# An fp32 hybrid-attention layer on one core: the first rows read in another order, two squares on VectorE, the second mean's chain given out sooner, and twelve weights kept as halves

## The chip, the cores and the metric

The kernel runs on one core of one Trainium2 chip. The metric is the device time of one execution in microseconds. Five engines work side by side, each on its own in-order queue: TensorE (PE, with PEld for its weight loads), VectorE (DVE), ScalarE (ACT), GpSimd (POOL) and SyncE (SP), which here only issues DMAs; GpSimd issues DMAs as well.

## The reference

One layer for 2048 prompt tokens and 32 sample tokens of width 1024 (2080 columns), all in float32:

```python
h = rmsnorm(x, ln_g)                                   # needs the mean of x*x of each token
q, k, v, gate_a, b_gate, c_gate, u_in, gate_c, merge_a, merge_c = split(h @ w_in)
attn, new_k, new_v = attend(rope(rmsnorm(q)), rope(rmsnorm(k)), v, sink)   # windows of 3 chunks of 64
y_a = (attn * silu(gate_a)) @ w_attn_out               # W_A
y_c = (b_gate * conv3(c_gate * u_in) * silu(gate_c)) @ w_conv_out          # W_B
r = x + (sigmoid(merge_a) * y_a + sigmoid(merge_c) * y_c) @ w_o            # O
out = r + sigmoid(r @ w_ple_gate) * (p @ w_ple_proj)   # PG and pp
```

It returns out, the rolled key and value rows, and the last two rows of the convolution's input.

## The kernel before, in words

**Arithmetic.** A float32 product is made of three fast products: each operand is split into a high half (a cast, on ScalarE) and a low half (the operand minus its high half, on VectorE), and TensorE adds high by high, high by low and low by high. The big products go over 2 by 2 blocks with 7 products instead of 8 (Strassen's scheme); for that, sums of four blocks of a weight are made on VectorE and kept in DRAM (`ws`, `qs`), and sums of blocks of the tokens are made the same way (`s`, `T`, `X`).

**Stages.** Times are those of the profiled execution.

- 0 to about 85 us, the start. The rows of p, four pieces of W_pp (`wpp_piece`, L931: raw tile `wppr`, halves `wpp_h` and `wpp_l`), the constants and x (`x_row`, L943) are loaded by SyncE. TensorE makes pp = p @ W_pp for blocks 0 and 1 while the mean of the first 512 tokens is worked out, then the first products of W_in. `x_row(j, k)` loads rows k of part j, squares them on ScalarE (`sq`) and adds the squares on VectorE into `sq_0`. When eight are added, `stats(j)` (L962) goes: eight one-column matmuls `pr` on TensorE, `rs` on VectorE, the power -1/2 on GpSimd, the diagonal `dg` on VectorE, four transposes `rps` on TensorE, a copy `rb` on ScalarE, and then the norms `b<-b,cst,rb`, x's halves and, for the second part (j = 1), the block sums (`combos` L1017, `make0` L1028). `sums0` (L1043) makes the weight sums of the first group and stores four of them.
- To about 440 us, the products of W_in in the first half of the tokens. They follow a list of steps, each of a dozen 128x512 matmuls (L1255 on). Beside them run extra pieces of work tied to the numbers of steps: sums of quads of W_o and W_pg (`quad_sums`, L375, at the steps of `sums_at`).
- About 440 to 860 us, the second half's products. Rows of x come back from DRAM (`refill`, L603; `refill_set`, L629: `xr`), weights come as `wr`. In this stage `half_steps` (L389) loads weights of W_A and the four sums of each O column one at a time, splits them (cast on ScalarE, subtraction on VectorE) and stores both halves in DRAM; `stored(key)` (L410) tells later stages that such a weight is loaded as halves and needs no split.
- 861 us to the end, attention (`attention`, L1399), yB, yA, the rest of pp, and the products O and PG (`big_x` L1705, `run_big` L1863; their sums are the tile `b`).

**What sets the order.** In the start and the last stage a planner runs while the program is written out. It has a clock of its own (`now`), a price for each instruction (`cost`, L104), and a queue of pieces of work with a due time and a rank. `go(g, us, need, rank)` (L184) gives out a generator; whenever TensorE's written work has moved on, `due` (L197) issues those that are due and whose buffers are free, by rank. An Engine object records every call, so all the planner's instructions have the line L160. Loads of the start come from a list, `todo_loads` (L1086), one after the other as SyncE's queue is free. In the last stage `next_loads` (L1994) orders weight loads and splits ahead of the product that runs; a weight is split once its load has landed by the planner's clock and ScalarE is not booked beyond a limit (L2044). Pieces of attention are begun `PRE` = 8 us ahead of their place (L2107). In between (85 to 860 us) the order is that of the list of steps.

Each engine runs what it got in that order, so a piece that waits holds what is behind it on its own engine.

Lines that the steps below touch (numbers of the profile):

```python
112            if key == "G":
113                return 2.03 if kw.get("op") == ALU.pow else 0.35 + 0.0021 * n
946        yield {"k": 1, "@": "S"}
948        eS.activation(out=sq, in_=v[:, :q0], func=AF.Square, scale=1.0 / 32.0)
953            yield {"@": "V"}
954            eV.tensor_tensor(out=acc0[j], in0=acc0[j], in1=sq, op=add)
958        if ready[j] == 8:
959            go(stats(j), now[0] + 1.8, None, j * 2 - 3)
1055        for p, i in WS.items():
1056            eG.dma_start(out=wsum[0][:, i], in_=sums[0][p])
```

## Time and profile before

| | us |
|---|---|
| three runs | 1509.11, 1510.27, 1509.16 |
| median | 1509.16 |
| the profiled execution | 1508.07 |
| its span, first to last instruction | 1506.0 |
| TensorE busy in it | 1489.3, 9553 matmuls |
| VectorE, ScalarE, GpSimd busy | 1210.7, 803.7, 399.0 |
| mean granted clock of TensorE | 0.998 |

How to read the rows quoted below. A row of the timeline is: start, length, engine, line, operation, output <- inputs (tile names without their numbers), shape, and how many such instructions follow each other; in brackets the idle time ahead of it and what ended that. The length of a group of several is from the first's start to the last's end. A matmul's length includes its way through the array, so the pace is read from start to start. A row of the waits is: who waited, for what, total, times, the longest. "SPq" is SyncE's queue: the issue of a DMA, not its transfer.

### The profile page before, as it was taken

The page shows a single profiled execution, that of the slowest core. Times are in us where ns is not written, and L with a number is a line of the kernel's source. Part 1 is how long each engine was busy: PE and PEld are TensorE (multiplying, and loading weights), DVE is VectorE, ACT ScalarE, POOL GpSimd, SP SyncE. Part 2 cuts the span into 40 slices and gives each one's busy share as a digit, 9 for nine tenths or more (in the row PEclk, how much of TensorE's full clock was granted, in tenths as well). Part 3 has the DMA queues.
Part 4 walks back from the last instruction along what each step waited for, and adds up shares of the span by engine and source line. Part 5 has one row for each costly group of instructions (what it writes and reads, how often), then busy time and mean ns, then how long its engine had stood idle before and what let it go on. Part 6 is the DMA issues. An engine that isn't in the chain of part 4 may idle for free.

```text
span 1506.0 us, 28005 instructions
## 1 busy us (share of the span) xinstructions
PE 1489.3 (99%) x9553; PEld 1348.6 (90%) x9553; DVE 1210.7 (80%) x2308; ACT 803.7 (53%) x1910; POOL 399.0 (26%) x582
## 2 busy tenths in 40 slices
PE   9999999999999999999999999999999999999998
PEld 7878888888889999999999989998888788999998
DVE  7897887885579788799976878778899999676777
ACT  8453244344457655434455646687765686342453
POOL 2133332332211443433323311113232202211201
PEclk9999999999999999999999999999999999999999
DMA  9469886898777987533578885687988959989959
GB/s 353 154 246 348 314 291 221 276 347 271 253 274 256 340 292 262 186 127 122 153 243 312 288 270 181 210 253 218 302 207 272 240 157 258 312 247 283 256 168 286
DMA packets 206670, 378.34 MB, mean 251 GB/s; under 512 B 24896, under 2 KB 58496, under 8 KB 206528
## 3 DMA queue, kind: packets, MB, share of 16 engines
q1 hardware_dynamic: 160608, 258.30, 52.6%
q0 software_dynamic: 36272, 100.44, 22.2%
q10 hardware_dynamic: 9648, 17.83, 3.2%
q8 instruction: 75, 1.23, 0.3%
q14 instruction: 67, 0.55, 0.1%
HBM read 246.53 MB, written 130.04 MB: 250 GB/s over the span
## 4 chain that ended last, share of the span: by engine, by line
PE 91%; DMA 4%; DVE 2%; ACT 1%; issue 1%; POOL 0%; SPq 0%; DVEq 0%; ACTq 0%; POOLq 0%
PE b L160 21%; PE a L654 8%; PE a L651 7%; PE a L649 7%; PE yB L160 6%; PE yA L160 5%; PE la L787 5%; PE c L651 4%; PE c L649 4%; PE c L654 4%; PE lc L787 2%; PE pp L160 2%; PE O L160 2%; PE S L160 2%; PE PT L160 1%; PE lb L787 1%
## 5 line engine op out<-in xcount | busy, mean ns | idle before, releaser
L160 PE MATMUL b<-xb_h,w 128*128 128x264 f32 (+1 forms) x1344 | 310.7, 322 | 1.4 <-DVE at L160 1.4
L160 PEld LDWEIGHTS b<-xb_h,w 128*128 128x128 f32 x1344 | 222.7, 188 | 19.5 <-DVE at L160 1.9
L651 PE MATMUL a<-x_l,w 128*128 128x264 f32 (+1 forms) x744 | 228.2, 320 | 0.0
L649 PE MATMUL a<-x_h,w 128*128 128x264 f32 (+1 forms) x744 | 227.4, 320 | 0.2 <-ACT w L231 0.2
L160 PE MATMUL b<-xb_l,w 128*128 128x264 f32 (+1 forms) x672 | 216.6, 322 | 0.0
L654 PE MATMUL a<-x_h,w 128*128 128x264 f32 (+1 forms) x744 | 199.7, 321 | 0.9 <-DVE w L232 0.9
L231 ACT CAST w<-wr 128x512 fp32r<-128x512 f32 (+1 forms) x180 | 110.5, 619 | 96.2 <-PE c L654 34.9
L232 DVE TENSOR_TENSOR w<-wr,w 128x512 fp32r<-128x512 f32 (+1 forms) x180 | 133.2, 748 | 29.6 <-ACT w L231 28.0
L649 PEld LDWEIGHTS a<-x_h,w 128*128 128x128 f32 x744 | 139.9, 188 | 11.3 <-ACT w L231 0.4
L651 PEld LDWEIGHTS a<-x_l,w 128*128 128x128 f32 x744 | 140.0, 188 | 10.9
L654 PEld LDWEIGHTS a<-x_h,w 128*128 128x128 f32 x744 | 124.0, 188 | 11.9 <-DVE w L232 1.2
L160 PEld LDWEIGHTS b<-xb_l,w 128*128 128x128 f32 x672 | 126.4, 188 | 8.5
L160 ACT CAST w<-wr 128x512 fp32r<-128x512 f32 x120 | 73.6, 622 | 98.4 <-PE b L160 51.5
L787 PE MATMUL la<-x_h,w 128*128 128x264 f32 x516 | 111.3, 285 | 1.6 <-ACT w L231 1.6
L651 PE MATMUL c<-x_l,w 128*128 128x512 f32 (+1 forms) x336 | 110.9, 340 | 0.0
L649 PE MATMUL c<-x_h,w 128*128 128x512 f32 (+1 forms) x336 | 110.5, 339 | 0.0
L231 ACT CAST w<-a 128x512 fp32r<-128x512 f32 x82 | 49.8, 620 | 98.6 <-DVE a L364 33.2
L654 PE MATMUL c<-x_h,w 128*128 128x512 f32 (+1 forms) x336 | 100.1, 339 | 0.0
L160 DVE TENSOR_TENSOR w<-wr,w 128x512 fp32r<-128x512 f32 x120 | 83.6, 705 | 18.0 <-ACT w L160 17.7
L848 DVE SCALAR_TENSOR_TENSOR u<-u,c 128x264 f32<-128x264 f32 (+1 forms) x125 | 59.5, 507 | 42.8 <-ACT u L843 26.1
L160 PE MATMUL yB<-ycs_h,w 128*128 128x264 f32 (+1 forms) x384 | 91.0, 325 | 0.0
L160 PE MATMUL yA<-ac_h,w 128*128 128x264 f32 (+1 forms) x384 | 90.5, 323 | 0.0
(443 smaller groups left out, 3889.7 us busy)
## 6 DMA issues: line engine op xcount, KB each, us to landing
wr<-in_wu SPq DMA_DIRECT2D x161, 256.0 KB, 4.8
a<-in_wu SPq DMA_DIRECT2D x116, 256.0 KB, 5.3
wr<-ws SPq DMA_DIRECT2D x74, 256.0 KB, 4.0
w<-o SPq DMA_DIRECT2D x32, 512.0 KB, 4.7
ws<-a POOLq DMA_DIRECT2D x63, 256.0 KB, 4.3
w<-wa SPq DMA_DIRECT2D x16, 512.0 KB, 5.3
wr<-qs SPq DMA_DIRECT2D x32, 256.0 KB, 4.0
qs<-a POOLq DMA_DIRECT2D x24, 256.0 KB, 5.8
```

Source lines behind the costliest of these rows:

```text
L160: return f(**kw)
L231: nc.scalar.copy(out=hi, in_=src)
L232: nc.vector.tensor_tensor(out=lo, in0=src, in1=hi.bitcast(F32), op=sub)
L649: nc.tensor.matmul(out=ps[:, :cn], lhsT=w[:, 0, k], rhs=x[0][:, c0:c0 + cn], start=first and k == 0, stop=False, skip_group_check=True)
L651: nc.tensor.matmul(out=ps[:, :cn], lhsT=w[:, 0, k], rhs=x[1][:, c0:c0 + cn], start=False, stop=False, skip_group_check=True)
L654: nc.tensor.matmul(out=ps[:, :cn], lhsT=w[:, 1, k], rhs=x[0][:, c0:c0 + cn], start=False, stop=k == 3, skip_group_check=True)
L787: nc.tensor.matmul(out=ps[:, :m], lhsT=w[:, a, k], rhs=r[:, cols], start=q in "ABG" and j == 0 and e == 0, stop=j == 1 and e == 2, skip_gr ...
L848: nc.vector.scalar_tensor_tensor(out=t[:, c0:c0 + cn], in0=t[:, c0:c0 + cn], scalar=-1.0, in1=ps[:, :cn], op0=mul, op1=sub)
```

## The change

Six edits:

- **The start's loads.** The fourth W_pp piece goes ahead of x rows 6 and 7 instead of behind them, the two rows of p's second block ahead of the first two weights, and all W_pp pieces get rank -3. The squares of x rows 2 and 5 of the first part are made on VectorE (x / 1024 times x) instead of ScalarE.
- **The second mean.** `stats(j)` is given out 0.3 us instead of 1.8 us after the last sum; this holds for both means. The planner's price for the power on GpSimd falls from 2.03 to 1.1.
- **The stores of the weight sums** go out one at a time, each when GpSimd is free and with rank 2, instead of four in a row.
- **Twelve weights as halves.** The weights (O, 1), (O, 4) and (PG, 1) of each of four columns n are loaded, split and stored as halves beside the steps of the first half, from the products of group 14 to the last group; in the last stage each of them is loaded as halves, 512 KB, with no split. A piece's four parts come 4 steps and 1 step ahead of its place, at it, and 0.4 steps behind.
- **The split condition.** A weight that is needed next may be split though ScalarE is booked up to 5.0 us ahead (before 1.5).
- **Attention** begins its first three pieces 11 us ahead instead of 8.

```diff
+H0 = 14
@@ cost
-            return 2.03 if kw.get("op") == ALU.pow else 0.35 + 0.0021 * n
+            return 1.1 if kw.get("op") == ALU.pow else 0.35 + 0.0021 * n
@@
+    RAW = {1: 0, 4: 1}
+    halves0 = {(x, n, p): dram.tile([P, 2, 4 * P], F32, tag=f"r{x}{n}_{p}", name=f"r{x}{n}_{p}")
+               for x, p in ((UO, 1), (UO, 4), (UPG, 1)) for n in range(4)}
@@ half_steps
+            elif key in halves0:
+                u, e = key[0] + key[1] + 4 * (key[2] == 4), RAW[key[2]]
+                nc.sync.dma_start(out=t.rearrange("p (a b) -> p a b", a=4), in_=wu[u, :, 4 * e:4 * e + 4, :])
@@ stored
+        if key[0] == "B" and key[1] == 0:
+            return halves0.get(key[2:])
@@ wpp_piece
-        go(hilo0(...), None, None, -3 if h < 2 else -1)
+        go(hilo0(...), None, None, -3)
@@ x_row
-        yield {"k": 1, "@": "S"}
+        vector = j == 0 and k in (2, 5)
+        yield {"k": 1, "@": "V" if vector else "S"}
         sq = row(f"sq{j}_{k}")[:, :q0]
-        eS.activation(out=sq, in_=v[:, :q0], func=AF.Square, scale=1.0 / 32.0)
+        if vector:
+            eV.scalar_tensor_tensor(out=sq, in0=v[:, :q0], scalar=1.0 / 1024.0, in1=v[:, :q0], op0=mul, op1=mul)
+        else:
+            eS.activation(out=sq, in_=v[:, :q0], func=AF.Square, scale=1.0 / 32.0)
...
-            go(stats(j), now[0] + 1.8, None, j * 2 - 3)
+            go(stats(j), now[0] + 0.3, None, j * 2 - 3)
@@ sums0
-        for p, i in WS.items():
-            eG.dma_start(out=wsum[0][:, i], in_=sums[0][p])
+        kept = dict(sums[0])
+
+        def keep():
+            for p, i in WS.items():
+                eG.dma_start(out=wsum[0][:, i], in_=kept[p])
+                yield {"@": "G"}
+        go(keep(), None, None, 2)
@@ todo_loads
-    todo_loads += [({}, (-2, x_row(0, k))) for k in range(3, 8)] + [({"wf": 1}, (-1, wpp_piece(3)))]
-    todo_loads += [({"wf": 1}, (0, raw0(i))) for i in range(2)] + [({"tmp": 1}, (0, p_row(1, k))) for k in range(2)]
+    todo_loads += [({}, (-2, x_row(0, k))) for k in range(3, 6)] + [({"wf": 1}, (-2, wpp_piece(3)))]
+    todo_loads += [({}, (-2, x_row(0, k))) for k in (6, 7)] + [({"tmp": 1}, (-1, p_row(1, k))) for k in range(2)]
+    todo_loads += [({"wf": 1}, (0, raw0(i))) for i in range(2)]
@@ the list of steps
+    gen0 = [half_steps(*x) for x in halves0.items()]
+    first0, last0 = at_step[0, H0, 7], at_step[0, G - 1, 5]
+    pitch0 = (last0 - first0) / (len(gen0) - 1)
+    at0 = sorted((first0 + pitch0 * j + lag, j) for j in range(len(gen0)) for lag in (-4, -1, 0, 0.4))
...
+        while at0 and at0[0][0] <= i:
+            next(gen0[at0.pop(0)[1]])
@@ next_loads
-                if landed.get(i, 1e9) > now[0] or busy["S"] >= now[0] + (0.3 if i > used[0] + 2 else 1.5):
+                if landed.get(i, 1e9) > now[0] or busy["S"] >= now[0] + (0.3 if i > used[0] + 2 else 1.5 if i > used[0] + 1 else 5.0):
@@ attention's begin
-        begin.append((max(0.0, t - PRE), lambda e=e, t=t: go(attention(e, t), None, {"z": 1, "tmp": 2})))
+        begin.append((max(0.0, t - (PRE if e > 2 else 11.0)), lambda e=e, t=t: go(attention(e, t), None, {"z": 1, "tmp": 2})))
```

What this does to the written order is shown at three places. (The changed file's lines stand one to thirteen further down: L161 is L160, L618 is L609, L353 is L352, L455 is L446.)

VectorE in the first 17 us, before. `wpp_l` is the low half of a W_pp piece (`wppr_260` the third, `wppr_272` the fourth), `sq_0` the sum of squares:

```order
L160 TENSOR_TENSOR sq_0_302<-sq_0_302,sq_1_307 128x512
L160 TENSOR_TENSOR sq_0_302<-sq_0_302,sq_2_311 128x512
L160 TENSOR_TENSOR wpp_l<-wppr_260,wpp_h 128x512
L160 TENSOR_TENSOR sq_0_302<-sq_0_302,sq_3_325 128x512
L160 TENSOR_TENSOR sq_0_302<-sq_0_302,sq_4_356 128x512
L160 TENSOR_TENSOR sq_0_302<-sq_0_302,sq_5_363 128x512
L160 TENSOR_TENSOR sq_0_302<-sq_0_302,sq_6_368 128x512
L160 TENSOR_SCALAR cst<-cst 128x64
L160 TENSOR_TENSOR sq_0_302<-sq_0_302,sq_7_374 128x512
L160 TENSOR_TENSOR wpp_l<-wppr_272,wpp_h 128x512
```

The same place after (`wppr_272` is now the third piece, `wppr_280` the fourth; `b_2` and `b_5` are x rows):

```order
L161 SCALAR_TENSOR_TENSOR sq_2_323<-b_2_270 128x512
L161 TENSOR_TENSOR sq_0_314<-sq_0_314,sq_1_319 128x512
L161 TENSOR_TENSOR sq_0_314<-sq_0_314,sq_2_323 128x512
L161 TENSOR_TENSOR wpp_l<-wppr_272,wpp_h 128x512
L161 TENSOR_TENSOR sq_0_314<-sq_0_314,sq_3_337 128x512
L161 SCALAR_TENSOR_TENSOR sq_5_375<-b_5_278 128x512
L161 TENSOR_TENSOR sq_0_314<-sq_0_314,sq_4_368 128x512
L161 TENSOR_TENSOR sq_0_314<-sq_0_314,sq_5_375 128x512
L161 TENSOR_TENSOR wpp_l<-wppr_280,wpp_h 128x512
L161 TENSOR_TENSOR sq_0_314<-sq_0_314,sq_6_389 128x512
L161 TENSOR_SCALAR cst<-cst 128x64
L161 TENSOR_TENSOR sq_0_314<-sq_0_314,sq_7_397 128x512
```

Two squares are new in this queue, and the fourth piece's low half stands two sums further up. On TensorE the eight matmuls `pr` move one place down, behind the fourth of the fourth piece's matmuls instead of the third.

VectorE at the second mean, 47 to 57 us, before. `rs`, `dg` are the mean's chain, `s` sums of products, `w` low halves of weights, `b` the norm of x rows:

```order
L160 TENSOR_SCALAR rs_1_720<-pr_1_721 128x4
L523 MEMSET rs_0_2062 128x5
L160 TENSOR_TENSOR s_0_642<-2_0_637,s_0_642 128x512
L160 TENSOR_TENSOR s_1_663<-2_1_638,s_1_663 128x512
L160 TENSOR_TENSOR w_738<-wr_455,w_738 128x512
L160 TENSOR_TENSOR w_742<-wr_680,w_742 128x512
L160 TENSOR_TENSOR w_744<-wr_688,w_744 128x512
L160 TENSOR_TENSOR s_2_669<-2_2_639,s_2_669 128x512
L160 COPY dg_1_778<-rs_1_720 128x512
L523 MEMSET rs_1_2410 128x5
L160 TENSOR_TENSOR s_3_766<-2_3_764,s_3_766 128x512
L160 SCALAR_TENSOR_TENSOR b_0_337<-b_0_337,cst,rb_1_792 128x512
```

After:

```order
L161 COPY dg_1_753<-rs_1_731 128x512
L532 MEMSET rs_1_2422 128x5
L161 TENSOR_TENSOR s_0_664<-2_0_659,s_0_664 128x512
L161 TENSOR_TENSOR s_1_687<-2_1_660,s_1_687 128x512
L161 TENSOR_TENSOR w_759<-wr_484,w_759 128x512
L161 TENSOR_TENSOR w_763<-wr_702,w_763 128x512
L161 TENSOR_TENSOR w_770<-wr_710,w_770 128x512
L161 TENSOR_TENSOR s_2_692<-2_2_661,s_2_692 128x512
L161 SCALAR_TENSOR_TENSOR b_0_349<-b_0_349,cst,rb_1_783 128x512
L161 SCALAR_TENSOR_TENSOR b_4_357<-b_4_357,cst,rb_1_783 128x512
L161 TENSOR_TENSOR s_3_798<-2_3_793,s_3_798 128x512
```

The diagonal moved from behind the six operations to ahead of them, and two norms stand ahead of `s_3`. On TensorE one of pp's products of block 1 (six 128x512 matmuls) now stands ahead of these products.

SyncE around 487 us, before. `wr` are weights, `xr` x rows:

```order
L352 DMA wr_5094<-in_wu 128x512
L352 DMA wr_5146<-in_wu 128x512
L352 DMA wr_5229<-in_wu 128x512
L609 DMA xr_0_4999<-xc_0_191 128x528
L609 DMA xr_1_5005<-xc_1_192 128x528
L609 DMA xr_2_5011<-xc_2_193 128x528
L609 DMA xr_3_5017<-xc_3_194 128x528
```

After:

```order
L353 DMA wr_5190<-in_wu 128x512
L353 DMA wr_5242<-in_wu 128x512
L618 DMA xr_0_5095<-xc_0_203 128x528
L618 DMA xr_1_5101<-xc_1_204 128x528
L618 DMA xr_2_5107<-xc_2_205 128x528
L618 DMA xr_3_5113<-xc_3_206 128x528
L353 DMA wr_5325<-in_wu 128x512
```

The third weight load moved behind the four row loads. Between these places and the last stage TensorE's rows stand in the same order from 519 to 1072 us, and SyncE's from 505 to 1052 us; after that twelve casts and twelve subtractions of weights are gone from ScalarE and VectorE, and pieces of attention stand at other places among the rest.

More of the change, by code (lines that the diff above doesn't have):

```diff
@@ L935, in wpp_piece @@
         wpp[h] = pair(f"wpp{h}")
-        go(hilo0(wpp[h][0][:, :512], wpp[h][1][:, :512], raw.rearrange("p a b -> p (a b)"), ("wpp", h), lambda: free("wf")), None, None, -3 if h < 2 else -1)
+        go(hilo0(wpp[h][0][:, :512], wpp[h][1][:, :512], raw.rearrange("p a b -> p (a b)"), ("wpp", h), lambda: free("wf")), None, None, -3)
     def constants():
```

## The prediction

> **What bounds the kernel now.** I read the page first: TensorE is busy for all but about 1% of the span, so nothing that shortens another engine's work shortens the kernel, unless TensorE waits for it.
>
> ```profile
> span 1506.0 us, 28005 instructions
> PE 1489.3 (99%) x9553; PEld 1348.6 (90%) x9553; DVE 1210.7 (80%) x2308; ACT 803.7 (53%) x1910; POOL 399.0 (26%) x582
> ```
>
> The change leaves the matmuls alone: the same products, in the same number. What it can win is what TensorE loses, and the view of TensorE's waits lists that by releaser (total, times, longest).
>
> ```profile
> PE la L787 <- ACT w L231: 1.6, 2, 1.1
> PE warm L1213 <- DVE ms L543: 1.5, 1, 1.5
> PE b L160 <- DVE at L160: 1.4, 1, 1.4
> PE pp L160 <- ACT wpp_h L160: 1.4, 1, 1.4
> PE pq L160 <- DMA zq<-z_q: 1.2, 1, 1.2
> PE 1_0_461 L649 <- ACT x_h L160: 1.0, 1, 1.0
> PE lc L787 <- ACT w L231: 1.0, 3, 0.4
> ```
>
> These seven make 9.1 us. A second kind of loss doesn't show there: a lower clock. The timeline of TensorE at the start, and the windows behind it (span; busy time of PE, PEld, DVE, ACT, POOL; granted clock; DMA share; GB/s), show both kinds one after the other.
>
> ```profile
> 13.79 0.40 PE L160 MATMUL pp<-p_l,wpp_h 128*128 128x512 f32 x1
> 14.02 0.39 PE L160 MATMUL pp<-p_h,wpp_l 128*128 128x512 f32 x1
> 15.79 0.50 PE L160 MATMUL pp<-p_h,wpp_h 128*128 128x512 f32 x1 [1.38 <-ACT wpp_h L160]
> 16.86 0.95 PE L160 MATMUL pr<-ones,sq 128*128 128x1 f32 x8
> 17.66 0.50 PE L160 MATMUL pp<-p_h,wpp_h 128*128 128x512 f32 x1
> 17.98 0.61 PE L160 MATMUL pp<-p_l,wpp_h 128*128 128x512 f32 x1
> 21.63 0.39 PE L160 MATMUL pp<-p_l,wpp_h 128*128 128x512 f32 x1
> 18.00:20.00 2.00, 2.00 (x6) 1.61 (x5) 1.81 (x4) 1.70 (x4) 1.46 (x3) 0.50 1.05 405
> 20.00:22.00 2.00, 2.00 (x7) 1.52 (x7) 1.03 (x2) 0.57 (x2) 0.56 (x1) 0.65 1.05 418
> ```
>
> At its pace a 128x512 matmul follows the last after 0.23 us (13.79 to 14.02). From 14.02 to 15.79 are 1.77 us, so 1.54 are lost to the wait for the fourth W_pp piece. Then the granted clock is 0.50 from 17.98: nine steps to 21.63 take 3.65 us instead of 2.10, another 1.55 lost. By the second window 0.35 x 2.00 / 0.50 = 1.4 us of it were slow, so the slow stretch is 2.0 + 1.4 = 3.4 us long. The prize at the start is 3.1 us if both go.
>
> **The start: x rows and squares.** What feeds the wait (timelines of VectorE, ScalarE, SyncE):
>
> ```profile
> 9.55 1.49 DVE L160 TENSOR_TENSOR sq<-sq,sq 128x512 f32<-128x512 f32 x2 [0.64 <-ACT sq L160]
> 12.60 2.29 DVE L160 TENSOR_TENSOR sq<-sq,sq 128x512 f32<-128x512 f32 x3 [0.31 <-ACT sq L160]
> 14.80 0.19 DVE L160 TENSOR_SCALAR cst<-cst 128x64 f32<-128x64 f32 x1
> 14.98 0.69 DVE L160 TENSOR_TENSOR sq<-sq,sq 128x512 f32<-128x512 f32 x1
> 15.77 0.69 DVE L160 TENSOR_TENSOR wpp_l<-wppr,wpp_h 128x512 fp32r<-128x512 f32 x1
> 22.73 1.90 DVE L160 TENSOR_TENSOR w<-wr,w 128x512 fp32r<-128x512 f32 x3 [1.51 <-ACT w L160]
> 10.25 0.62 ACT L160 CAST wpp_h<-wppr 128x512 fp32r<-128x512 f32 x1
> 15.12 0.62 ACT L160 CAST wpp_h<-wppr 128x512 fp32r<-128x512 f32 x1
> 10.24 1.00 SPq L160 DMA_DIRECT2D wr<-in_wu  x2
> 12.94 2.25 SPq L160 DMA_DIRECT2D wr<-in_wu  x4
> ```
>
> SyncE's issue at 10.24 goes out as the third piece's cast starts (10.25): an issue waits for the landing eight places ahead, so the issues give the landings, about 0.67 us apart (1.00 - 0.33). The fourth piece moves two places up the queue: from the landing that released the third of the issues from 12.94 on (14.3) to that of the first (12.9). ScalarE, relieved of two squares, casts it at 12.95 to 13.57 instead of 15.12 to 15.74. So far 2.2 us are won on the wait.
>
> But two squares join VectorE's queue, and its order (shown with the change) puts both ahead of the fourth piece's subtraction. From the rows, independent operations start (1.90 - 0.68) / 2 = 0.61 us apart, sums on the same tile (2.29 - 0.69) / 2 = 0.80. Counted on from the square at 9.57: sum1 10.25, sum2 11.04, third wpp_l 11.65, sum3 12.27, square five 12.89, sum4 13.57, sum5 14.36, fourth wpp_l 14.97 to 15.66, sum6 15.59, the constants' scaling 16.21 (they now land as the 17th transfer, about 16.1), sum7 16.38 to 17.07. TensorE can start the fourth piece's first two matmuls at 14.25 and 14.48, then waits for wpp_l until 15.69, does two more, and reaches the eight one-column matmuls pr, which now wait for sum7 until 17.1 and take 0.80 (16.86 to 17.66). It goes on at 17.9, where before it went on at 17.98. The wait for ScalarE is replaced by two for VectorE of about 1.0 and 0.9 us. The half clock I expect again, since there is as little matmul time ahead of it. Term: 0.0. Bounds: -3.1 (VectorE keeps up, both losses go) and +0.7 (one transfer more ahead of the constants, pushing sum7 by a landing).
>
> **The second mean.** Its chain ends in TensorE's wait at 84.62.
>
> ```profile
> 51.83 0.42 DVE L160 COPY dg<-rs 128x512 f32<-128x512 f32 x1
> 54.60 0.60 PE L160 MATMUL rps<-cst,dg 128*128 128x128 f32 x4
> 55.53 0.69 DVE L160 TENSOR_TENSOR s<-2_3_764,s 128x512 f32<-128x512 f32 x1 [3.15 <-issue]
> 82.21 0.68 DVE L160 TENSOR_TENSOR b<-b,b 128x512 f32<-128x512 f32 x1
> 84.62 0.50 PE L649 MATMUL 1_0_461<-x_h,w 128*128 128x512 f32 x1 [1.02 <-ACT x_h L160]
> ```
>
> In the new order the copy `dg` stands right behind `rs` instead of behind three sums and three subtractions, so it starts at about 48.8, and the transposes at about 51 instead of 54.60. That is 3.5 us at the head of the chain. But VectorE then does two norms and meets the sum `s_3`, whose product on TensorE ends 1.40 us later than before (six 128x512 matmuls of the second block's pp now stand ahead: 6 x 0.233). So `s_3` starts at about 56.9 instead of 55.53, with everything behind it. Counting the 40 operations from there to the `b` of 82.21 at 0.62 gives 81.7: only 0.5 of the 3.5 us is left. The wait of 1.02 shrinks by as much. Term: -0.5; bounds -1.0 (all gone) and +0.6 (the stores of the weight sums, which no longer go out together, and the weight sums themselves come late behind x's splits; one operation's length).
>
> **The row reload at 487.**
>
> ```profile
> 484.75 3.37 SPq L352 DMA_DIRECT2D wr<-in_wu  x3
> 488.17 1.86 SPq L609 DMA_DIRECT2D xr<-xc  x4
> 498.19 0.39 PE L787 MATMUL la<-x_h,w 128*128 128x264 f32 x1 [0.43 <-ACT w L231]
> ```
>
> The third `wr` waits 3 us on SyncE's queue for a buffer, and four row loads stand behind it; the order now has the rows ahead of it, so they go about 2 us sooner. ScalarE's casts of the rows and weights behind them were late by 0.43 at 498.19 and by up to 0.4 three times in the `lc` row above. Term: -0.6; bounds -1.1 and 0. The waits before (`la` 1.1) lie ahead of the moved loads and stay.
>
> **Twelve weights kept as halves.** In the first half come 12 loads of 256 KB, 12 casts, 12 subtractions and 24 stores on GpSimd's queue; in the last phase 12 casts and 12 subtractions go, and 12 loads are twice as large. The windows of the two places:
>
> ```profile
> 300.00:325.00 25.00, 25.00 (x109) 20.20 (x108) 21.80 (x35) 9.87 (x18) 10.23 (x19) 1.00 0.96 338
> 1100.00:1150.00 50.00, 50.00 (x270) 41.99 (x269) 49.53 (x100) 30.27 (x89) 13.82 (x14) 1.00 0.84 238
> 1200.00:1250.00 50.00, 48.58 (x264) 41.11 (x264) 47.25 (x92) 41.63 (x117) 4.58 (x4) 1.00 0.56 162
> 1203.47 0.42 DVE L160 TENSOR_TENSOR at<-O,ga 128x256 f32<-128x256 f32 x1
> ```
>
> In the first half TensorE lost nothing (25.00 of 25.00) while VectorE was busy 21.80 of 25 and the DMA engines 0.96: 12 x 0.69 = 8.3 us of VectorE and 12 x 0.62 = 7.4 us of ScalarE, spread over some 130 us, fit into what those two leave free (3.2 us in this 25, on ScalarE 15). What hides them is that slack; the loads are asked for three steps (36 matmuls of 0.233 us, 8.4 us) ahead of the cast. Term: +0.3, a wait of the smallest kind above; bounds 0 and +6 (the slower rival below).
>
> In the last phase VectorE is nearly full (49.53 of 50), and its late `at` at 1203.47 is TensorE's wait of 1.4. Twelve subtractions less are 12 x 0.69 = 8.3 us less there, far more than 1.4, but the planner spends part of it: it starts attention pieces earlier and packs them closer. Term: -1.2, nearly the whole wait; bounds -2.6 (this and the other small waits of the phase, as long again) and +1.4 (an equal collision elsewhere).
>
> The earlier start of the first three attention pieces (11 instead of 8 us) I cost at nothing, neither gain nor loss: the rows of TensorE from 519 to 1072 us and of SyncE from 505 to 1052 us stand as before, so `pq`'s wait for its DMA (1.2 in the table) stays. Likewise the planner's smaller price for the power operation and its looser condition for casts add no instruction; they act through the orders above.
>
> **Sum.** 0.0 - 0.5 - 0.6 + 0.3 - 1.2 = -2.0 us. The profiled execution took 1508.07 us (span 1506.0 and 2.07 around it), 1.09 below the median of 1509.16; so I expect 1506.1 for such an execution and 1507.2 on the median's footing.
>
> **The rivals.**
>
> *VectorE keeps up at the start* (0.15). Its chain hangs on two landings that I place by the 0.67 us of a row: x row two's (9.57) and the constants' (16.1). The constants are small (128x64) and may land ahead of their place; if row two is there two places (1.3 us) sooner as well, the fourth wpp_l ends by 14.4 and sum7 by 15.8. Then TensorE waits some 0.5 us ahead of pr and no more, and the half clock doesn't come: 3.1 - 0.5 = 2.6 better, 1507.2 - 2.6 = 1504.6. Against it: VectorE's first sum waited 0.64 for ScalarE's square at 9.55, so the rows were not there early.
>
> *The wait stays, the half clock goes* (0.12). The slow stretch is 3.4 us long and begins at 17.98, 3.4 us after the last full matmul before the wait (14.02 + 0.39 = 14.41). The wait of 1.4 at `b`, in the window from 1200, left the clock at 1.00, so a wait alone doesn't halve it; the one-column matmuls next to it, or where in a fixed grid of 3.4 us the wait falls, do. With the wait split in two (1.0 and 0.9, two matmuls between), a grid may cut it: 1507.2 - 1.55 = 1505.65. [...]
>
> *The kept weights cost* (0.10, slower). Their raw loads come in a stretch with DMA at 0.96 (338 GB/s; the start reached 418). ScalarE takes its queue in order: a cast whose load has not landed 8.4 us after its issue holds the weight casts behind it, and TensorE waits as it does in the rows for ScalarE's `w`, 0.52 a time (`la` 1.6 in 2 and `lc` 1.0 in 3). Twelve such make 6.2: 1507.2 - 0.3 + 6.2 = 1513.1. It decides from the point where a load takes over 8.4 us. Against it: TensorE waits for nothing in that window today. For it: VectorE and the DMA engines are near full there.
>
> *The last phase gains nothing* lies inside the forecast: with 0 or +1.4 for -1.2 it gives 1508.4 or 1509.8.
>
> **Chances and range.** A measurement of this kernel can tell about 0.2% (3.0 us) from no change: faster means below 1506.1, slower above 1512.2. My forecast has 0.63; its terms' bounds put about a fifth of that (0.13) below 1506.1. The first rival is nearly all faster (0.13 of 0.15), the second about half (0.07 of 0.12), the third mostly slower (0.08 of 0.10): faster 0.33, slower 0.08, the same 0.59. The range goes down to the first rival with the last phase at its lower bound (1504.6 - 1.4 = 1503.2) and up to the forecast with the start at +0.7, the second mean at +0.6 and the last phase at 0 (1507.2 + 0.7 + 1.1 + 1.2 = 1510.2); it leaves out the slower rival and a tail below, while the 1509.8 of the last phase at +1.4 lies in it.
>
> **What would show it.** Right: in the start a wait of `pp` for VectorE's wpp_l near 14.7 to 15.7 and one of `pr` for `sq` near 16 to 17, a clock of 0.50 in one window of 16 to 22; the transposes `rps` near 51 with VectorE's `s_3` near 57; the wait at 84 about half; no wait at 498; `pq` still 1.2; no `b` wait for `at`; TensorE full from 300 to 430. Wrong: no wait between 14 and 18 with a clock of 1.00 throughout (first rival), a chain of `w` casts waiting for the copies' loads between 300 and 430 (third), or new waits for VectorE between 1050 and 1330.

## The result, and the profile after

The changed kernel takes 1526.23 us (median of 4 runs, 1524.33 to 1529.73), the kernel before beside it 1509.13: a ratio of 1.0117, 95% interval 1.0096 to 1.0137. The forecast was 1507.2 with a range up to 1510.2; the measured time lies far above both, and above the slower rival (1513.1) too. The profiled execution has a span of 1524.4 us. Two executions of the sets below were in a slow state (2073.64 us with the copies alone, 2958.22 us of the kernel before) and count in none of the ratios.

The page after shows as many matmuls, less work on VectorE and ScalarE than before, and still a longer span.

```profile
span 1524.4 us, 28080 instructions
PE 1497.0 (98%) x9553; PEld 1352.8 (89%) x9553; DVE 1202.9 (79%) x2310; ACT 801.8 (53%) x1908; POOL 409.7 (27%) x606
```

The waits of TensorE after (total, times, longest), the largest groups:

```profile
PE O L161 <- DVE ptl L161: 6.2, 1, 6.2
PE b L161 <- DVE c L161: 4.0, 1, 4.0
...
PE pq L161 <- DMA zq<-z_q: 1.4, 1, 1.4
PE a L658 <- ACT u L852: 1.2, 1, 1.2
PE pr L161 <- DVE sq L161: 1.0, 1, 1.0
```

Three that the prediction meant to remove are gone or smaller: `pp` for `wpp_h`, `1_0` for `x_h`, `b` for `at`. In their place stand two waits, 6.2 and 4.0 us, longer than any before (1.5), both in the last phase, and a new one (`a` for `u`) at the end of the first half. The chain of waits into the first long one, from a load and the issue of a store on:

```profile
1179.76 8.12 DMA w<-r
...
1187.94 12.19 DMA z_r<-c
...
1200.25 0.70 DVE c L161
...
1202.27 0.34 DVE kr L161
...
1203.21 0.34 DVE ptl L161
...
1203.60 0.58 PE O L161
```

By the profile, a store of a result row (`z_r<-c`) was held in SyncE's queue until a load of a kept weight (`w<-r`), eight issues ahead of it, had landed after 8.12 us (in this trace each of the 972 issues of the queue behind the first eight starts after the landing of the one eight issues ahead, 115 of them within 0.15 us). Issued at 1187.94, the store lands 12.19 us later. VectorE's next `c` needs that row's buffer, and VectorE ran its queue in the written order: behind `c` (started at 1200.25) came `kr` (1202.19), `qr` (1202.53) and `ptl` (1203.13) of an attention piece, which TensorE waited for. VectorE's timeline shows the hole:

```profile
1200.25 0.69 DVE L161 TENSOR_TENSOR c<-c,c 128x512 f32<-128x512 f32 x1 [8.69 <-DMA z_r<-c]
```

Why the store was late shows in the view of the DMAs between 1160 and 1200 us (MB in the stretch; then each kind of issue: count, KB each, median us to landing). The windows before had room only in the second half of it (DMA share next to last):

```profile
1160.00:1180.00 20.00, 20.00 (x109) 16.87 (x108) 17.04 (x32) 14.33 (x46) 6.12 (x7) 1.00 1.07 306
1180.00:1200.00 20.00, 20.00 (x106) 16.89 (x105) 19.79 (x40) 12.35 (x33) 6.04 (x8) 1.00 0.87 209
```

The DMAs before:

```profile
DMA packets 7326, 10.29 MB, mean 257 GB/s; under 512 B 1140, under 2 KB 3103, under 8 KB 7322
...
z_r<-c SPq DMA_DIRECT2D x11, 256.0 KB, 4.2
...
wr<-qs SPq DMA_DIRECT2D x9, 256.0 KB, 4.1
```

After:

```profile
DMA packets 7126, 12.44 MB, mean 311 GB/s; under 512 B 1152, under 2 KB 2717, under 8 KB 7121
...
w<-r SPq DMA_DIRECT2D x8, 512.0 KB, 8.5
...
z_r<-c SPq DMA_DIRECT2D x8, 256.0 KB, 6.6
wr<-qs SPq DMA_DIRECT2D x8, 256.0 KB, 9.3
```

Eight of the twelve kept weights (`w<-r`, 512 KB) are loaded in these 40 us. Before, one raw load of those weights (`wr<-in_wu`, 256 KB) lay here; the others had gone out from 1134 us on, as raw weights have buffers of their own and are fetched eleven weights ahead. A weight kept as halves goes straight into the buffer of a split weight, and that comes free late. So the change doubles the bytes of these eight and moves them into 40 us that were nearly full, and what stood there slows down: weight sums from 4.1 to 9.3 us, stores from 4.2 to 6.6 and in one case to 12.2.

The second long wait is another case. VectorE stands at a `c` that needs the buffer of a store of the output (`out_yT<-c`), 70 us after the last kept weight was loaded (1190.99):

```profile
1270.85 0.69 DVE L161 TENSOR_TENSOR c<-c,b 128x512 f32<-128x512 f32 x1 [6.91 <-DMA out_yT<-c]
...
1271.59 0.80 PE L161 MATMUL b<-xb_h,w 128*128 128x512 f32 x1 [3.96 <-DVE c L161]
```

That store took 10.02 us. The stores `out_yT` between 1235 and 1290 us before:

```profile
DMA to landing us min/median/max: 4.9/6.3/12.2
```

Before, the longest took even more, VectorE waited 4.6 us for one of them at another place (`xb_l`), and TensorE was not held. So a later landing does not explain the second wait; what stands behind that store in VectorE's new order is left as its cause.

The clock of TensorE falls with the long waits (the trace records half clock from 1202.57 to 1209.39 and from 1270.83 to 1277.66 us); the windows around them, after:

```profile
1200.00:1250.00 50.00, 46.40 (x234) 39.35 (x235) 44.37 (x84) 35.37 (x100) 4.97 (x5) 0.93 0.54 164
1250.00:1300.00 50.00, 46.04 (x258) 40.04 (x258) 39.49 (x75) 31.58 (x80) 9.63 (x12) 0.93 0.86 222
```

0.93 over 50 us is 0.07 x 50 / 0.50 = 7 us at half clock, in each window, and half of that is lost. How the loss is shared out: `pq`, at 888.01 before, starts at 890.89 (2.9 us late); the last matmul, at 1499.65 before, starts at 1518.43. So 2.9 us came in the first 890 us and 18.78 - 2.88 = 15.9 behind them: the two waits and the half clock of both windows.

```profile
890.89 0.63 PE L161 MATMUL pq<-cst,zq 128*128 128x128 f32 x4 [1.38 <-DMA zq<-z_q]
1518.43 0.29 PE L161 MATMUL b<-xb_h,w 128*128 128x264 f32 x1
```

The start went as replayed. TensorE and VectorE there, after:

```profile
15.11 0.50 PE L161 MATMUL pp<-p_h,wpp_l 128*128 128x512 f32 x1
16.80 1.02 PE L161 MATMUL pr<-ones,sq 128*128 128x1 f32 x8 [0.95 <-DVE sq L161]
17.68 0.48 PE L161 MATMUL pp<-p_l,wpp_h 128*128 128x512 f32 x1
14.37 0.69 DVE L161 TENSOR_TENSOR wpp_l<-wppr,wpp_h 128x512 fp32r<-128x512 f32 x1
...
18.00:20.00 2.00, 2.00 (x6) 1.52 (x5) 1.67 (x5) 1.27 (x3) 1.82 (x2) 0.53 1.07 412
```

The wait for `wpp_h` is gone, a wait of 0.95 for the sum of squares stands in its place, TensorE goes on at 17.68 (17.98 before, 17.9 forecast), and the clock is halved again from 18 us on.

### The profile page after: what moved, and what is told of

Read it like the earlier page. It is cut to its first block, busy times and chain, and to the rows that moved or that the text cites. A ratio compares the mean times of both kernels' runs of the same rounds, so it can differ in the third digit from the quotient of the medians.

```text
span 1524.4 us, 28080 instructions
## 1 busy us (share of the span) xinstructions
PE 1497.0 (98%) x9553; PEld 1352.8 (89%) x9553; DVE 1202.9 (79%) x2310; ACT 801.8 (53%) x1908; POOL 409.7 (27%) x606
## 4 chain that ended last, share of the span: by engine, by line
PE 81%; DMA 7%; DVE 4%; issue 4%; ACT 2%; POOL 1%; SPq 0%; ACTq 0%; DVEq 0%; POOLq 0%
PE b L161 17%; PE a L663 7%; PE a L658 7%; PE a L660 7%; PE yA L161 6%; PE yB L161 6%; PE la L796 5%; PE c L658 3%; PE c L660 3%; PE c L663 3%; PE lc L796 2%; PE O L161 2%; PE S L161 2%; PE pp L161 2%; DMA z_r<-c 1%
## 5 line engine op out<-in xcount | busy, mean ns | idle before, releaser
L161 PE MATMUL b<-xb_h,w 128*128 128x264 f32 (+1 forms) x1344 | 312.5, 324 | 5.0 <-DVE c L161 4.0
L161 PEld LDWEIGHTS b<-xb_h,w 128*128 128x128 f32 x1344 | 224.0, 190 | 23.9 <-DVE c L161 4.4
L161 PE MATMUL b<-xb_l,w 128*128 128x264 f32 (+1 forms) x672 | 217.9, 324 | 0.0
L161 PEld LDWEIGHTS b<-xb_l,w 128*128 128x128 f32 x672 | 127.3, 189 | 8.9
L161 ACT CAST w<-wr 128x512 fp32r<-128x512 f32 x108 | 66.7, 623 | 97.7 <-PE b L161 53.4
L161 PE MATMUL yB<-ycs_h,w 128*128 128x264 f32 (+1 forms) x384 | 90.9, 325 | 0.0
L161 PE MATMUL yA<-ac_h,w 128*128 128x264 f32 (+1 forms) x384 | 90.4, 323 | 0.0
L796 PEld LDWEIGHTS la<-x_h,w 128*128 128x128 f32 x516 | 86.5, 188 | 2.7 <-ACT w L232 2.0
```

The costliest lines, as they stand in the source:

```text
L161: return f(**kw)
L796: nc.tensor.matmul(out=ps[:, :m], lhsT=w[:, a, k], rhs=r[:, cols], start=q in "ABG" and j == 0 and e == 0, stop=j == 1 and e == 2, skip_gr ...
```

## The experiments

My theory after the result: the reading of the kept weights costs by its bytes. Its rival: the planner, with twelve splits fewer, packs the last phase closer, and VectorE asks for buffers too early whatever the loads carry. A third question is what the copies of the first half cost. All medians stand beside the kernel before on the same chip, as a ratio with its 95% interval. The runs were taken on several chips, on which the kernel before differs by up to 1.0 us (1508.64 to 1509.65), so a difference between medians of two runs is good to about 1 us.

**Without any kept weight.**

```diff
-        while at0 and at0[0][0] <= i:
-            next(gen0[at0.pop(0)[1]])
...
-        if key[0] == "B" and key[1] == 0:
-            return halves0.get(key[2:])
```

> The change without the twelve kept weights: they are neither split ahead nor loaded as halves; all else as after. Both theories (bytes of the larger loads; the planner's new order of the last phase) put the loss into the kept weights and expect 1507 to 1509.5, with no wait of TensorE over 2 us after 1000 us and a clock of 1.00 there. If other parts of the change carry it (the split condition, attention's earlier begin, the second mean), it stays above 1515.

Measured: 1507.49 (before 1508.64), ratio 0.9993 (0.9984 to 1.0003). So the other five edits together are worth about -1.1 us, not clear of nothing. The waits of this kernel:

```profile
PE lc L794 <- ACT w L232: 1.8, 3, 1.2
...
PE b L161 <- DVE at L161: 1.4, 1, 1.4
PE pq L161 <- DMA zq<-z_q: 1.3, 1, 1.3
```

No long wait is left. VectorE's late `at` (1.4) is back, and so are the waits around 490 (`lc` 1.8): the new order of the row loads at 487 us came from the copies, not from the other edits.

**The copies alone.** Only the second pair of lines above is taken out: the halves are stored, and nobody reads them.

> The twelve weights are loaded, split and stored beside the first half as after, but the last phase does not read them: it loads them raw and splits them again. It separates what the copies cost in the first half from what the reading costs. The after trace lost 3.1 us between 400 and 450 us where before lost nothing: I expect 2 to 3.5 us more than without any kept weight, 1510 to 1512.5. If the copies cost nothing, as forecast (+0.3), it equals that kernel within 1 us.

Measured: 1513.24 (before 1508.64), ratio 1.0029 (1.0018 to 1.0039). The copies cost 1513.24 - 1507.49 = 5.8 us, more than either number expected. Not all of it lies beside the copies: `pq`, at 888.04 without kept weights, starts at 891.03, 3.0 us late, and behind its wait (1.8) came half clock (0.83 from 890 to 900 us, 3.4 us of it at half), another 1.7 us, which the execution without kept weights did not have (1.00 there). What is left of the change, reading the halves, costs 1526.23 - 1513.24 = 13.0.

**The kept weights alone, on the kernel before** (the lines of `halves0`, `half_steps`, `stored` and the list of steps from the change, nothing else).

> The kernel before with the twelve kept weights as its only change. If they carry the loss by themselves, 1525 to 1528; if they only lose together with the looser split condition and the new price of the power operation, 1510 to 1518.

Measured: 1531.34 (before 1509.11), ratio 1.0143 (1.0126 to 1.0161). They lose by themselves, 22 us, 3 to 4 more than inside the full change (18.7); the loss doesn't need the other edits. The largest wait of TensorE is a new one here, 4.9 us at 452.84 for ScalarE's `w`, behind two row loads `xr<-xc` that took 5.4 and 7.0 us.

**The reading alone.**

```diff
-        while at0 and at0[0][0] <= i:
-            next(gen0[at0.pop(0)[1]])
...
-        if key[0] == "B" and key[1] == 0:
-            return halves0.get(key[2:])
+        if key[0] == "B" and key[1] == 0 and key[2:] in halves0:
+            return halves["o", key[3], 7]
```

> The change without the copies of the first half; the last phase loads the twelve weights as halves of 512 KB each, in the same order on every engine as after, from halves of other weights that are stored anyway (so the products use wrong weights). Copies cost 5.8 us in the run before (1513.2 against 1507.5): if copies and reading add, this gives 1526.2 - 5.8 = 1520.5, with both long waits of TensorE. If the copies' delay is what sets off the waits of the last phase, below 1513.

Measured: 1522.44 (before 1509.11), ratio 1.0086 (1.0070 to 1.0101). That is 15 us over the kernel without kept weights. 15.0 and 5.8 make 20.8 where both together cost 18.7 (1526.23 - 1507.49): nearly additive. The reading needs no help from the copies.

**The same order with half the bytes.**

```diff
-                W2[i] = w[:, 0], w[:, 1]
-                eY.dma_start(out=w.bitcast(F32).rearrange("p a b c -> p a (b c)"), in_=src)
+                if worder[i][0] == "B" and worder[i][1] == 0 and worder[i][2:] in halves0:
+                    W2[i] = w[:, 0], w[:, 0]
+                    eY.dma_start(out=w[:, 0].bitcast(F32).rearrange("p b c -> p (b c)"), in_=src[:, 0])
...
```

> The order of the instructions is that of after on every engine; only the loads of the twelve kept weights carry 256 KB (the high half, which TensorE then uses in place of the low half too) instead of 512 KB. It leaves out the low halves of twelve weights. Bytes theory: the stores z_r land in about 5 us again, the waits of 6.2 and 4.0 us and the half clock behind each go: 1526 - 10.5 - 3 = about 1512.5. Order theory: VectorE still asks for the buffers too early, the waits stay: 1523 to 1526.

Measured: 1517.83 (before 1508.64), ratio 1.0060 (1.0042 to 1.0078). Between the two expectations: 8.4 us go, and 4.6 over the copies alone stay. The stores `z_r` between 1160 and 1215 us, first in the after kernel, then here: who waited for their landing, and how long that took.

```profile
  DVE c L161: 8.7, 1
...
DMA to landing us min/median/max: 3.1/5.5/12.2
```

```profile
  DVE c L161: 4.2, 1
...
DMA to landing us min/median/max: 3.1/5.8/8.6
```

The longest landing falls from 12.2 to 8.6, VectorE's wait from 8.7 to 4.2. With as many bytes as raw weights have, the loads still come in the same 40 us, not spread from 1134 on. But a late landing alone isn't enough. The same stores in the kernel before, for which nobody waited:

```profile
DMA to landing us min/median/max: 2.3/4.1/9.2
```

9.2 us cost nothing there, and 8.6 cost VectorE 4.2 us here. So it also counts how soon the buffer is asked for again, which the order of the last phase sets.

**The same order with an eighth of the bytes** (the copy's target and source cut to one block, `w[:, 0, 0]` from `src[:, 0, :P]`).

> As after, copies included and with the same order on every engine, but the loads of the twelve kept weights carry 64 KB each (one of the high half's four blocks, which TensorE uses in place of all eight). It leaves out the rest of these weights. With half the bytes the time was 1517.8, 4.6 above that of the copies alone (1513.2). If that rest is still bytes landing late, it goes: 1512 to 1514.5. If it is the new order of the last phase, it stays: 1516.5 to 1519.

Measured: 1515.43 (before 1509.11), ratio 1.0046 (1.0031 to 1.0061); its runs spread from 1511.24 to 1519.90. The profiled execution is the fastest of them. In it the longest landing is 7.3, nobody waits for a `z_r` store, and the first long wait is gone; the second is shorter but stays:

```profile
DMA to landing us min/median/max: 3.1/5.2/7.3
...
1258.09 0.69 DVE L161 TENSOR_TENSOR c<-c,b 128x512 f32<-128x512 f32 x1 [4.72 <-DMA out_yT<-c]
```

TensorE loses 1.8 us there. So with the order unchanged, 10.8 of the 13.0 us of the reading (1526.2 - 1515.4) go with the bytes. The second wait comes with the order: none of the kernels that load these weights raw has it, though their longest `out_yT` landings are 11.2 to 12.9 us. The last 2.2 us fit it, but the median lies between the two expectations and the spread of these runs covers it; how much the order costs by itself stays open.

**The stores on another queue.** The reading alone again, with `z_r` issued by GpSimd.

```diff
-            eY.dma_start(out=z_r[k][:, cols], in_=t)
+            Engine("Y", nc.gpsimd).dma_start(out=z_r[k][:, cols], in_=t)
```

> The reading alone (1522.4), with the stores z_r issued from GpSimd's queue instead of SyncE's, where they stand behind the 512 KB loads; the order on the other engines is the same. It uses wrong weights as the run of the reading alone. If the stores land late because they stand behind the big loads on one queue, both long waits shrink: 1511 to 1515. If the DMA engines themselves are full, it stays: 1520 to 1525.

Measured: 1518.35 (before 1509.65), ratio 1.0061 (1.0039 to 1.0083): 4 us better than the reading alone, and between the two expectations. The wait of TensorE for `ptl` shrinks (the reading alone lost 5.4 us there, this one 2.7), the second long wait stays (2.5 and 2.6). The landings of the `z_r` stores hardly change (longest 11.7 in the reading alone and 10.0 here, median 6.0 and 6.2), while VectorE's wait for one falls from 9.6 to 3.2. So part of the lateness is the place behind the big loads on SyncE's queue, and part is the slow landing, which the store meets on GpSimd's queue too.

**Four kept weights.** `halves0` holds only (O, 1).

```diff
-               for x, p in ((UO, 1), (UO, 4), (UPG, 1)) for n in range(4)}
+               for x, p in ((UO, 1),) for n in range(4)}
```

> The change with four kept weights, those of O's first product, instead of twelve. Their loads fall at 1091 to 1105 us, where the DMA engines are not full; the eight that fell between 1166 and 1191 are raw again. Bytes theory: no wait over 2 us after 1000, a third of the copies' cost: 1507 to 1510.5. Order theory: a third of the loss or an arbitrary part of it: 1510 to 1520.

Measured: 1515.48 (before 1508.64), ratio 1.0048 (1.0029 to 1.0067). Four kept weights cost 8.0 us over none, where twelve cost 18.7: more than a third, and against the bytes theory's number. Its two largest waits:

```profile
PE la L796 <- ACT x_h L232: 3.3, 1, 3.3
PE b L161 <- DVE c L161: 2.2, 1, 2.2
```

The first is at 436 us, where the row loads for the second half come late; the second at 1242. Neither goes by the number of weights; where the pieces fall counts as much as how many they are. The four loads themselves cost nothing: from 1090 to 1110 us, where they fall, the DMA share is 1.06 (0.72 before), and TensorE is busy 19.74 of 20 us in both.

**The copies earlier.** The copies alone, ending two groups of products earlier (five groups for twelve copies instead of seven).

```diff
-    first0, last0 = at_step[0, H0, 7], at_step[0, G - 1, 5]
+    first0, last0 = at_step[0, H0, 7], at_step[0, G - 3, 5]
```

> The copies alone (the last phase loads the weights raw), given out up to two groups earlier, so that the last of them lies ahead of the change from the first half's products to the second's at 433 us. If the copies cost by pushing the row loads and ScalarE's output copies at that change, the waits at 433 to 446 (3 us) go: 1508.5 to 1511. If they cost by their work and bytes anywhere, 1512.5 to 1514.

Measured: 1516.63 (before 1509.11), ratio 1.0049 (1.0034 to 1.0064). Worse, so my reason (the last copy in the way of the row loads) was wrong: packed closer, the copies cost more, though the last of them lies further ahead of the change of halves. SyncE's queue shows how it reaches there:

```profile
418.99 5.46 SPq L353 DMA_DIRECT2D wr<-in_wu  x2
...
436.35 0.85 SPq L647 DMA_DIRECT2D xr<-xc  x2
```

Weight loads wait up to some 5 us, one after the other, and the first row load behind them goes out at 436.35; without copies it goes out at 425.26.

**The copies at 200 to 290 us.**

```diff
-    first0, last0 = at_step[0, H0, 7], at_step[0, G - 1, 5]
+    first0, last0 = at_step[0, 7, 7], at_step[0, 12, 5]
```

> The copies alone (the last phase loads the weights raw), given out between about 200 and 290 us, where the DMA engines were busy 0.7 of the time before, instead of 303 to 440, where they were 0.97 in the first third. If the copies cost by filling the DMA engines until loads and buffers come late, the cost nearly goes: 1507 to 1509.5. If twelve more casts, subtractions and stores cost wherever they stand, it stays at 1512 to 1517.

Measured: 1514.15 (before 1509.65), ratio 1.0029 (1.0019 to 1.0038). The cost moves with them; no better place was found by going where the DMA engines were 0.7 busy. It now shows as `a` waiting for VectorE's `w` and for `u` between 244 and 308:

```profile
PE a L661 <- DVE w L233: 2.5, 2, 1.7
PE a L656 <- ACT u L850: 1.8, 1, 1.8
```

**The copies without their stores.**

```diff
-        with in_turn(nc.gpsimd.engine):
-            nc.gpsimd.dma_start(out=dst[:, 0], in_=h.bitcast(F32))
-            nc.gpsimd.dma_start(out=dst[:, 1], in_=t)
+        if key not in halves0:
+            with in_turn(nc.gpsimd.engine):
+                nc.gpsimd.dma_start(out=dst[:, 0], in_=h.bitcast(F32))
+                nc.gpsimd.dma_start(out=dst[:, 1], in_=t)
```

> The copies alone at their place from 303 us on (the last phase loads the weights raw), with the 24 stores to DRAM left out: the loads, casts and subtractions stay, 6.3 of the 9.4 MB go, and the buffers come free without waiting for a store. If the stores (their bytes and their hold on the shared buffers) carry the cost of the copies, 1507.5 to 1510. If the loads and the work on ScalarE and VectorE carry it, 1512 to 1514.

Measured: 1508.01 (before 1509.42), ratio 0.9984 (0.9974 to 0.9993). The whole cost of the copies goes with their 24 stores, by the medians; the profiled execution is the slowest of its ten (1511.17) and doesn't show the gain. The window 350 to 400 us with the copies, and the same without the stores:

```profile
350.00:400.00 50.00, 50.00 (x217) 40.38 (x216) 31.74 (x56) 24.44 (x44) 18.02 (x34) 1.00 0.99 354
```

```profile
350.00:400.00 50.00, 50.00 (x217) 40.42 (x216) 32.70 (x55) 23.48 (x42) 12.89 (x24) 1.00 0.86 301
```

The DMA engines go from 0.99 to 0.86. Whether it is the bytes or the buffers that a store holds until it lands, this run doesn't separate; a copy with buffers of its own wasn't tried.

**Eight other weights.** The seventh and fifth products of PG, copied between about 230 and 310 us.

```diff
-               for x, p in ((UO, 1), (UO, 4), (UPG, 1)) for n in range(4)}
+               for x, p in ((UPG, 7), (UPG, 5)) for n in range(4)}
...
-                u, e = key[0] + key[1] + 4 * (key[2] == 4), RAW[key[2]]
-                nc.sync.dma_start(out=t.rearrange("p (a b) -> p a b", a=4), in_=wu[u, :, 4 * e:4 * e + 4, :])
+                nc.sync.dma_start(out=t, in_=quad_sum[UPG, key[1]][:, WS[key[2]]])
...
-    first0, last0 = at_step[0, H0, 7], at_step[0, G - 1, 5]
+    first0, last0 = at_step[0, 9, 7], at_step[0, 13, 5]
```

> The change with eight other kept weights, the seventh and fifth products of PG, copied between about 230 and 310 us and read as halves near 1180 to 1215 us, the end of the stretch in which DMA is full and the start of the one in which it was busy 0.3 to 0.5. Bytes theory: no wait over 2 us after 1000, the wait of 1.4 for VectorE at 1204 gone: 1505.5 to 1509. If reading halves costs by itself, with the load in place of a split asked for too late, over 1512.

Measured: 1507.67 (before 1509.65), ratio 0.9984 (0.9975 to 0.9994). So reading halves is not costly in itself; by these runs it depends on where the loads fall and what their order does behind them, which this run changes together. These eight loads go out from 1204.74 to 1241.44, later than expected, where the DMA share before was 0.56 (1200 to 1250), and neither long wait comes. This version beats both kernels, though by 0.16% against the kernel before, and against the change without kept weights (0.9993, 0.9984 to 1.0003) it can't be told apart. The wait for `at` is still 1.2 of 1.4 us. That says nothing on whether fewer subtractions would end it: VectorE's subtractions up to the `at` are the same as before, and the eight that went lay behind it, from 1216 us on.

## Why the prediction was wrong, point by point

**The failed step** is the sum of the twelve kept weights. The prediction named "12 loads are twice as large" and then priced only the casts and subtractions that go (-1.2, bounds -2.6 and +1.4). Bytes had no price, and the place of the loads wasn't looked at: eight of them move from 1134 on, where raw weights are fetched ahead, to 1166 to 1191, where DMA was already nearly full. Its own rows had the warning: a DMA share of 0.84 in the window from 1100 that it quoted for VectorE's sake. The runs put +13 to +15 us in place of -1.2, of which 10.8 go with the bytes. It was also wrong that VectorE's 8.3 us of freed time would be spent by the planner: VectorE had a hole of 8.69 us instead, as its queue stood behind one late store, and a second of 6.91. Of its signs of being wrong, "new waits for VectorE between 1050 and 1330" is the one that came. "An equal collision elsewhere" was priced at +1.4 at most; the second wait, which the new order makes, is such a collision, 4.0 us and half clock behind it.

**The copies** were priced at +0.3 by the slack of VectorE and ScalarE, and cost 5.8. The twelve casts and subtractions are indeed hidden, as forecast (without the stores nothing is lost). The term that was mis-sized is the 24 stores, which were counted as issues on GpSimd's queue and not as 6.3 MB at a DMA share near 1. The slower rival had the right place. Its mechanism, a load that lands late ahead of ScalarE's casts, is seen in part, on other loads than it named: the rows behind the copies came late (the 4.9 us on the kernel before). Whether the stores do that by their bytes or by holding buffers stays open.

**The start** came as replayed: the wait for ScalarE gone, VectorE's chain in its place. `pr` waited 0.95 (forecast 0.9), TensorE went on at 17.68 (17.9); only the wait for `wpp_l` was smaller (some 0.3 instead of 1.0), as VectorE's chain reached it at 14.37, 0.6 us sooner than counted. The half clock came again. By the rivals' terms neither of the two that promised a gain happened in this execution. Stretches in steps of 3.4 us, on which the second rests, are what the traces record (below); that the place of a wait among them decides over the half clock stays the prediction's assumption, as no run shows it. Its reading of the trace before was a little off: from the end of the last full matmul (14.41) to the half clock (17.98) are 3.6 us, not 3.4.

**The second mean** came as replayed too: `dg` at 48.53 (48.8), `rps` at 50.82 (about 51), `s_3` at 56.66 (56.9). The wait at 84 fell from 1.02 to 0.2, a gain of 0.8 and more than the -0.5; but a wait of 0.60 for ScalarE's `w` is new at 102.34, from the weight sums that were pushed back:

```profile
50.82 0.60 PE L161 MATMUL rps<-cst,dg 128*128 128x128 f32 x4
85.69 0.51 PE L660 MATMUL 1_0_471<-x_l,w 128*128 128x512 f32 x1 [0.20 <-DVE x_l L161]
102.34 0.50 PE L658 MATMUL c<-x_h,w 128*128 128x512 f32 x1 [0.60 <-ACT w L232]
```

**The row reload**: the waits at 494 and 498 went, as forecast, but through the copies; without them the order is as before and the waits stay. Booked under the wrong edit.

**What was to cost nothing** (attention's earlier begin, the split condition) cost nothing: with all of it in place and no kept weight the time is 1507.49, and `pq` still waits 1.3. Start, second mean and these together were forecast at -0.5, or -1.1 with the row reload; measured -1.1, with an interval of about -2.4 to +0.5. That -1.1 stands on both sides is luck in part: the row reload is in the forecast, and its waits stayed in that kernel.

## What to carry to other kernels

To replace work by a stored result, price the bytes first: what is written, what is read again, and the DMA share of the windows in which both will fall. Here a load that lost its fetch-ahead buffers also lost its early place, and fell into a fuller one. Ask also what the new order puts behind each store that reuses a buffer: landings of 10 to 12 us cost TensorE nothing in one order and 4 us in another. Here one late store was paid by the `c` that reuses its buffer (8.69 us of VectorE), and by what stood behind `c` on that queue, which was quite another chain (`ptl`, 6.2 us of TensorE).

## What the runs showed of the hardware

The stretches of one clock that the traces of before and after record are, but for the last of each, whole multiples of 3.413 us. Before: 13.65 us full (4 times), 3.41 half from 17.98 on, 1481.38 full (434 times). After: 13.65 full, 3.41 half from 18.14 on, 1181.01 full (346 times), then in the last phase 6.83 half twice (2 times each), with 61.44 full between (18 times). Without kept weights the eight warm-up matmuls took 3.62 us, against 2.81 before and 2.88 after, and with almost the same wait in the start as after (0.82, there 0.95) the clock stayed full:

```profile
2.48 3.62 PE L1230 MATMUL warm<-warm 128*128 128x256 f32 x8
16.36 1.02 PE L161 MATMUL pr<-ones,sq 128*128 128x1 f32 x8 [0.82 <-DVE sq L161]
18.00:20.00 2.00, 2.00 (x10) 1.62 (x9) 1.67 (x4) 1.71 (x4) 1.66 (x2) 1.00 1.06 414
494.00:498.00 4.00, 4.00 (x23) 4.00 (x22) 3.70 (x7) 3.32 (x9) 1.08 (x2) 0.57 0.85 253
```

The same execution then had 3.4 us at half clock from 494.5 on (0.43 x 4.00 / 0.50), behind waits of 1.17 and 0.30 us and with no one-column matmul beside them, while the wait of 1.38 for `pq` after and that of 1.4 for `at` before left the clock at 1.00. So in these executions a gap of little over a microsecond cost some 1.5 us more or nothing. What decides it the runs do not show. A gain that hangs on one such wait could not be forecast here for a single execution, only as a chance.
